# Splitting the next stage's first weights early, storing the residual tile by tile, and reordering the first norm, in a one-core hybrid decoder layer

## The chip, the cores and the metric

The kernel runs on one core of a Trainium2 chip, as a single program. The metric is the device time of one execution in microseconds (us). A core has five engines that matter here: PE (TensorE, matrix products), DVE (VectorE), ACT (ScalarE), POOL (GpSimd) and SP (SyncE, which in this kernel issues nearly all DMAs). Each engine takes its instructions in order; semaphores tie the engines together.

## The reference

The reference is one inference step of one decoder layer for 576 tokens: a prompt of 512 and eight samples of 8 tokens. The model width D is 1024, the feed-forward width 2816. In fp32 it computes

- `x = x + 1/2 * SwiGLU_1(rmsnorm(x))`, where `SwiGLU(h) = (silu(h @ w_gate) * (h @ w_up)) @ w_down`;
- `h = rmsnorm(x)`, `P = h @ w_in`: one projection that gives queries, keys and values of a dilated sliding-window attention (branch A) and of a gated linear attention (branch B), an output gate `rg` for B, and one gate for each branch;
- `m = sigmoid(g_a) * (A @ w_a_out) + sigmoid(g_b) * (B @ w_b_out)`, then `x = x + m @ w_out`;
- `x = x + 1/2 * SwiGLU_2(rmsnorm(x))`, and the new rows of the key-value caches and the new GLA states as further outputs.

`rmsnorm(x)` is `x * rsqrt(mean(x*x) + eps) * g`, row by row. B's output is multiplied by `silu(rg)`.

## The kernel before

**Tiling.** The residual x is kept transposed in SBUF: `xT` is 128 x 8 x 576, eight tiles of 128 features, and the 576 tokens are two HALVES of 288. A "group" is one output tile of 128 features for one half: eight k tiles, each with three matmuls of 128 x 128 by 128 x 288, so 24 matmuls. The three matmuls stand for one fp32 product: every fp32 operand is split into a high part (a cast to fp32r) and a low part (what the cast lost), and `feat_mm` adds high x high (L191), high x low (L192) and low x high (L193). Where the tokens are the rows of the result, L921 to L923 do the same (`ptok`). The larger part of the feed-forward products runs as `Unit`s, a Strassen scheme of seven half-size products (`Unit.products`, L521 to L523, results `pX`, `pY`, `pZ`).

**Weights.** A weight tile of 512 KB goes through `fetch_w` (DMA from SP's queue, L160, into a buffer `raw`), then `split`: ACT casts it (`wh`, L138), DVE subtracts (`wl`, L139). PE's L191 needs `wh`, its L193 needs `wl`. The buffers belong to a pool that is opened for each stage by `weights(raw_bufs, w_bufs, sums)`: 4 and 6 in the sublayers, 2 and 8 in the mixer and in the `w_out` loop. A new stage's pool lies where the old one lay, so its first fetch waits for what the old stage does there.

**Norms.** The 1/rms of a token is a factor of the whole row, so the products start with `x * g` (`operand`, L228 on ACT for the high and L229 on DVE for the low part) and each result is multiplied by `row`, which holds 1/rms of each token along the free axis. For a norm between stages `updated` runs for each (tile, half) of x as it becomes final: operand, square (L236, L238) and running sum (L239). After the sixteenth, `sums` adds over the partitions by matmuls with ones (`pssq`, L250), takes mean plus eps on DVE (`rms`, L207) and the power -1/2 on POOL (`rtok`, L208), and `rows_` spreads it by transposes on PE (`prow`, L221) and copies by ACT (`row`, L222).

**Order.** PE's order is the order of the code (the kernel is written under a manual schedule); a scheduler orders the other engines' instructions when the program is built. A small helper, `weave`, counts PE's groups: `weave.put_off(n, step)` puts a step n groups later, `weave.tick()` closes a group, and `weave.run` interleaves lists of groups and steps.

**Stages.** (1) *Start*: x is loaded as tokens x features, transposed by PE (`first_tokens`), the first norm's squares are summed per token (`first_squares`: chunks 0 to 2 by ACT at L333, 3 to 5 by DVE at L335), the root comes from POOL (`st`, L208), `first_rows` makes `row`. (2) *First sublayer*, `sublayer(E, xT, 1, ...)`: 16 groups of class `First` (mat 0 is gate, 1 is up; `evac` multiplies by `row` at L615 and L619, takes silu at L616 and the product at L621), while `normal_steps` makes the normed operands of the `Unit`s (`factor` at L575; L585, L586 and L591 combine them; `hop` are the split results); then `Unit`s for gate, up and down, and at the end `Last` groups (`pd`) whose results are added to x at L740 and handed to `after1`. When all sixteen are there, SP stores x to DRAM (`xsp`, L392) in two transfers, since the mixer needs the room. (3) *Mixer*: it opens with three tiles of the gate `rg`, all of half 0 first, then all of half 1 (`feat_groups`, results `pf`, evacuated by DVE at L966, two groups later); then attention (first result `ptok`), gated linear attention and the branches. ACT's silu of a gate tile (L994) needs both halves of it. (4) *`w_out` loop*: x is reloaded from `xsp`, eight tiles of `w_out` (results `pwo`) are added at L415 and go to `updated`. (5) *Second sublayer*, as the first, with its own weights, and output.

Of the kernel before, what the change touches and what calls it, by code (L numbers as in the profile page):

```python
# [9 lines left out]
F32 = mybir.dt.float32  # L10
# [88 lines left out]
def hybrid_step_kernel(  # L99
# [199 lines left out]
    for c in range(3, 6):  # L299
        load_x(c)  # L300

    fst = xi.tile([NC, 24], F32, tag="st1", name="st1", bufs=1)

    def first_columns():
        pc = ps_bg("pcols1")
# [23 lines left out]

    def first_squares(c):  # L330
        sq = xi.tile([NC, D], F32, tag="sqx", name="sqx", bufs=1)
        if c < 3:
            S.activation(sq, xt[c], AF.Square, accum_out=fst[:, c:c + 1])  # L333
        else:
            V.tensor_tensor_reduce(sq, xt[c], xt[c], op0=ALU.mult, op1=ALU.add, scale=1.0, scalar=0.0,  # L335
                                   accum_out=fst[:, c:c + 1])
        if c % 3 == 2:
            rstd_of(fst[:, 14 + c:17 + c], fst[:, c - 2:c + 1], fst[:, 6 + c:9 + c], D)

# [26 lines left out]
    def second():  # L366
        for c in range(3, 6):
            first_tokens(c)
        wpre[0, 1] = load_w([gv[:, :, P:2 * P]])
        for c in range(3):  # L370
            first_squares(c)

    weave.put_off(1, second)
    weave.put_off(2, lambda: first_operands(1))
    weave.put_off(2, lambda: [first_squares(c) for c in range(3, 6)])
    weave.put_off(4, lambda: (first_rows(0), E.scaled(0)))

    def last_rows():
        first_rows(1)
        start.close()  # L380
        other_columns()
        xin.close()
        E.scaled(1)

    weave.put_off(5, last_rows)
    seen = []

    def after1(m, h):
        updated(xT, m, h, 2, sacc[:, :T], sacc[:, T:], seen)
        if len(seen) == 2 * KD:  # L390
            for s in HALVES:
                SP.dma_start(xsp[:, :, s], xT[:, :, s])  # L392

    sublayer(E, xT, 1, ffn1_gate, ffn1_up, ffn1_down, wpre, after1)
    sub.close()
    wst.close()
    wst = weights(2, 8)
    mxs = ExitStack()
    mixer(E, mxs, bk, xpool)
    bk = banks(6)  # L400
    branches(E, mxs)

# [5 lines left out]
    ov = kview(w_out)  # L408
    for m in range(KD):
        w = load_w([ov[:, :, m * P:(m + 1) * P]])  # L410
        for h, s in enumerate(HALVES):
            po = ps_acc("pwo")
            feat_mm(po[:, :HALF], w, 0, P, E.mH, E.mL, range(KD), s)
            weave.tick()
            V.tensor_add(xT[:, m, s], po[:, :HALF], xT[:, m, s])  # L415
            updated(xT, m, h, 3, sacc[:, :T], sacc[:, T:], seen)
# [22 lines left out]
            q.dma_start(y_prompt[0, SEQ - 32:SEQ, c], y[:32, 2 * P:])  # L439
            q.dma_start(ys[:, c], y[32:, 2 * P:])  # L440

    sublayer(E, xT, 3, ffn2_gate, ffn2_up, ffn2_down, {}, lambda m, h: weave.put_off(1, lambda: out(m, h)))
    weave.finish()
    sub.close()
    wst.close()
# [78 lines left out]
        self.done(i, ps)  # L524


def sublayer(E, xT, g, wg, wu, wd, wpre, after):


    V, S, weave = E.V, E.S, E.weave  # L530
# [28 lines left out]
    normed = []  # L559

    def scaled(*halves):
        ready.update(halves)
        if len(ready) == 2:
            E.scaled = lambda *halves: None
            weave.put_off(1, normal)

    def normal():

# [31 lines left out]
        normed.extend((fn, k) for k in range(4) for fn in (lower, lower2, lower3))  # L600

    def normal_steps(n):
        for fn, *a in normed[:n]:
            fn(*a)
        del normed[:n]

    E.scaled = scaled
    ps = {}
# [41 lines left out]
            E.feat_mm(po[:, :HALF], wpre[mat, f], 0, P, E.hH, E.hL, range(KD), HALVES[h])  # L650
            waiting.append((mat, f, h, weave.at + 2))

    first = [First(*k) for k in ((0, 0, 0), (1, 0, 0), (0, 1, 0), (0, 0, 1), (1, 0, 1), (1, 1, 0), (0, 1, 1), (1, 1, 1))]
    first += [First(mat, f, h) for f in range(2, 2 * FIRST) for mat in range(2) for h in range(2)]


    def gate(pair):
# [87 lines left out]

    units = [fn(pair) for pair in phases[0][FIRST:] for fn in (gate, up)]
    for n, phase in enumerate(phases):
        nxt = phases[n + 1] if n + 1 < len(phases) else tail
        units.append(gate(nxt[0]))
        downs = [down(phase, m) for m in range(0, KD, 2)]  # L750
        rest = [up(nxt[0])] + [fn(pair) for pair in nxt[1:] for fn in (gate, up)]
        units += rest + downs if nxt is tail else downs + rest
    lasts = [Last(m) for m in range(0, KD, 2)]

    slots = [(-1, u, 0) for u in first]
# [30 lines left out]
    for i, (_, u, n) in enumerate(slots):  # L786
        ahead(i)
        u.products(n)
        weave.tick()
        evacuate(i)  # L790
        normal_steps(2)
        if not any(isinstance(x[1], Unit) for x in slots[i + 1:]):
            for x in final:
                after(*x)
            final.clear()
# [136 lines left out]
    return [loaded(load, group, t) for t in range(5)]  # L932


def feat_groups(E, c0, ms, evac, by_half=False):

    wv = E.kview(E.w_in)
    ws = {}

    def load(m, h):  # L940
        if m not in ws:
            ws[m] = E.load_w([wv[:, :, c0 + m * P:c0 + (m + 1) * P]])

    def group(m, h):
        s = HALVES[h]
        po = E.ps_acc("pf")
        E.feat_mm(po[:, :HALF], ws[m], 0, P, E.hH, E.hL, range(KD), s)
        if by_half:
            E.weave.put_off(2, lambda: evac(m, s, po[:, :HALF]))
        else:  # L950
            evac(m, s, po[:, :HALF])

    order = [(m, h) for h in range(2) for m in ms] if by_half else [(m, h) for m in ms for h in range(2)]
    return [loaded(lambda a=a: load(*a), group, *a) for a in order]


def mixer(E, mxs, bk, xpool):
    S, weave = E.S, E.weave
    E.mxl = mxs.enter_context(E.sb("mixl"))
    E.aH = E.mxl.tile([P, 2, T], F32R, name="aH")  # L960
# [4 lines left out]
    E.oT = oT = [E.slot(E.slotsA, F32, f"oT{m}") for m in range(KD)]  # L965
    gate_out = lambda m, s, ps: E.V.tensor_mul(oT[m][:, s], ps, E.row[:, s])  # L966

    weave.run(feat_groups(E, C_RG, range(3), gate_out, True))
    xpool.close()
    bk.close()  # L970
    bk = E.banks(4)
# [723 lines left out]
```

## Time and profile before

| what | value |
|---|---|
| median of 3 runs | 1450.68 us (1449.65 to 1452.04) |
| the profiled execution | 1450.8 us, its span 1449.0 us |
| PE busy | 1406.5 us, 97% of the span |
| DVE busy | 1066.9 us, 74% |
| ACT busy | 720.8 us, 50% |
| POOL busy | 58.7 us, 4% |
| DMA | 144.26 MB, mean 100 GB/s |
| mean granted PE clock | 0.989 of full speed |

The span is the time from the first to the last recorded instruction; the execution's own time has a little more around it. A row of the timeline gives the start in us, the duration, the engine, the line of the kernel, what is written and read, and in brackets the idle time of the engine before it with what ended it. A row of a window gives its bounds and length, the busy time of each engine with the number of instructions, the granted clock of PE as a share of full speed, the DMA engines' busy share and what they moved.

### The profile page before, as it was taken

How to read it: one execution, taken by the hardware profiler on the slowest of the kernel's cores; microseconds unless marked ns; L12 is line 12 of the kernel's file. 1: busy time of each engine (PE TensorE's matmuls, PEld its weight loads, DVE VectorE, ACT ScalarE, POOL GpSimd, SP SyncE). 2: the span in 40 equal slices, each digit the busy share in tenths (PEclk: the TensorE clock that was granted, in tenths of full speed). 3: DMA queues.
4: the chain of work that ended last, by engine and by line, in shares of the span. 5: the costliest groups of instructions: out<-in, count | busy, mean ns of one | idle time of the engine just before them, and what ended most of it. 6: DMA issues, size and time to landing. Idle time of an engine off the chain costs nothing.

```text
span 1449.0 us, 27438 instructions
## 1 busy us (share of the span) xinstructions
PE 1406.5 (97%) x10836; PEld 1374.3 (95%) x10836; DVE 1066.9 (74%) x2340; ACT 720.8 (50%) x1468; POOL 58.7 (4%) x89
## 2 busy tenths in 40 slices
PE   7989999999969999999999999999999999999998
PEld 7979999999959999998999999999999999999997
DVE  6999999998844456542477666555479999999892
ACT  6564664665533455632455644323345556556642
POOL 2000000000012212000000000000000000000000
PEclk9999999999979999999999999999999999999999
DMA  7223323332252442273324432325221333233232
GB/s 194 61 63 99 102 78 114 88 102 78 70 155 82 139 128 72 73 200 121 88 63 118 123 110 81 84 81 167 74 80 53 92 114 88 88 104 101 83 109 66
DMA packets 179951, 144.26 MB, mean 100 GB/s; under 512 B 7242, under 2 KB 178944, under 8 KB 179824
## 3 DMA queue, kind: packets, MB, share of 16 engines
q1 hardware_dynamic: 179488, 142.34, 33.7%
q8 instruction: 85, 1.39, 0.4%
q0 software_dynamic: 336, 0.18, 0.1%
q14 instruction: 42, 0.34, 0.1%
HBM read 128.72 MB, written 13.78 MB: 98 GB/s over the span
## 4 chain that ended last, share of the span: by engine, by line
PE 90%; DVE 5%; DMA 2%; ACT 1%; SPq 1%; issue 0%; POOL 0%; ACTq 0%; POOLq 0%; DVEq 0%
PE pX L523 8%; PE pX L522 8%; PE pX L521 8%; PE pY L522 4%; PE pY L523 4%; PE pY L521 4%; PE pf L191 4%; PE pf L193 3%; PE pf L192 3%; PE ptok L921 3%; PE ptok L923 3%; PE ptok L922 3%; PE pZ L522 2%; PE pZ L523 2%; PE pZ L521 2%; PE pg L191 1%
## 5 line engine op out<-in xcount | busy, mean ns | idle before, releaser
L138 ACT CAST w<-raw 128x512 fp32r<-128x512 f32 (+1 forms) x360 | 205.4, 578 | 123.6 <-PE pX L523 32.3
L139 DVE TENSOR_TENSOR w<-raw,w 128x512 fp32r<-128x512 f32 (+1 forms) x360 | 224.6, 635 | 21.1 <-ACT w L138 18.9
L521 PE MATMUL pX<-hop,w 128*128 128x288 f32 x576 | 170.1, 295 | 5.0 <-ACT w L138 5.0
L523 PE MATMUL pX<-hop,w 128*128 128x288 f32 x576 | 171.0, 297 | 3.0 <-DVE w L139 3.0
L522 PE MATMUL pX<-hop,w 128*128 128x288 f32 x576 | 170.8, 297 | 0.0
L138 ACT CAST wh<-raw 128x1024 fp32r<-128x1024 f32 (+2 forms) x111 | 106.7, 969 | 124.6 <-PE pf L192 46.6
L139 DVE TENSOR_TENSOR wl<-raw,wh 128x1024 fp32r<-128x1024 f32 (+2 forms) x111 | 124.0, 1125 | 46.2 <-ACT wh L138 45.7
L191 PE MATMUL pf<-h,wh 128*128 128x288 f32 x384 | 119.2, 310 | 13.9 <-ACT wh L138 13.9
L921 PE MATMUL ptok<-wl,h 128*128 128x256 f32 x416 | 120.1, 289 | 0.0
L923 PE MATMUL ptok<-wh,h 128*128 128x256 f32 x416 | 116.9, 281 | 0.0
L922 PE MATMUL ptok<-wh,h 128*128 128x256 f32 x416 | 116.7, 281 | 0.0
L193 PE MATMUL pf<-h,wl 128*128 128x288 f32 x384 | 114.8, 299 | 0.4 <-DVE wl L139 0.4
L192 PE MATMUL pf<-h,wh 128*128 128x288 f32 x384 | 114.6, 299 | 0.0
L521 PEld LDWEIGHTS pX<-hop,w 128*128 128x128 f32 x576 | 109.1, 189 | 5.7 <-ACT w L138 5.7
L523 PEld LDWEIGHTS pX<-hop,w 128*128 128x128 f32 x576 | 109.0, 189 | 4.3 <-DVE w L139 4.3
L522 PEld LDWEIGHTS pX<-hop,w 128*128 128x128 f32 x576 | 109.1, 189 | 0.0
L191 PEld LDWEIGHTS pf<-h,wh 128*128 128x128 f32 x384 | 73.9, 192 | 17.0 <-ACT wh L138 14.1
L522 PE MATMUL pY<-hop,w 128*128 128x288 f32 x288 | 85.1, 296 | 0.0
L523 PE MATMUL pY<-hop,w 128*128 128x288 f32 x288 | 85.0, 295 | 0.0
L521 PE MATMUL pY<-hop,w 128*128 128x288 f32 x288 | 84.6, 294 | 0.0
L191 PE MATMUL pg<-h,wh 128*128 128x288 f32 x256 | 79.1, 309 | 3.2 <-ACT wh L138 2.4
L921 PEld LDWEIGHTS ptok<-wl,h 128*128 128x128 f32 x416 | 78.6, 189 | 1.8 <-issue 1.3
(426 smaller groups left out, 4268.9 us busy)
## 6 DMA issues: line engine op xcount, KB each, us to landing
raw<-in_w_in_dram SPq DMA_DIRECT2D x58, 512.0 KB, 3.9
raw<-in_ffn_gate_dram SPq DMA_DIRECT2D x45, 512.0 KB, 3.8
raw<-in_ffn_up_dram SPq DMA_DIRECT2D x44, 512.0 KB, 3.8
raw<-in_ffn_down_dram SPq DMA_DIRECT2D x48, 384.0 KB, 3.2
raw<-in_ffn_down_dram SPq DMA_DIRECT2D x8, 512.0 KB, 3.6
kv<-in_cache_swa_kv_dram SPq DMA_DIRECT2D x32, 128.0 KB, 4.0
kv<-in_cache_swa_kv_dram SPq DMA_DIRECT2D x16, 256.0 KB, 4.3
S<-in_state_gla_dram SPq DMA_DIRECT2D x4, 1024.0 KB, 6.8
```

The lines of the kernel that those rows point to most:

```text
L138: S.copy(hi, src)
L139: V.tensor_sub(lo, src, f32(hi))
L191: PE.matmul(ps, h, ah, start=first and j == 0, stop=False)
L192: PE.matmul(ps, h, al, start=False, stop=False)
L193: PE.matmul(ps, l, ah, start=False, stop=last and j == n - 1)
L521: PE.matmul(ps, wh[:, k], ah, start=opens and k == 0, stop=False, skip_group_check=True)
L522: PE.matmul(ps, wh[:, k], al, start=False, stop=False, skip_group_check=True)
L523: PE.matmul(ps, wl[:, k], ah, start=False, stop=k == self.nk - 1, skip_group_check=True)
L921: PE.matmul(po[:, :256], ah, wl, start=(k == 0), stop=False)
L922: PE.matmul(po[:, :256], al, wh, start=False, stop=False)
L923: PE.matmul(po[:, :256], ah, wh, start=False, stop=(k == KD - 1))
```

## The change

It has five parts.

1. *Start*: the sums of squares lie in `sacc` instead of a tile of their own; all six squares are ACT's; the second half's operands come in two pieces, before and after squares 0 to 2; squares 3 to 5 are put off by three groups, and the second half's row by six instead of five.
2. *Residual*: `after1` stores each (tile, half) of x as soon as it is final, 16 stores of 144 KB from POOL's queue (L394 of the changed kernel), instead of two stores of 1152 KB from SP's queue after all of them.
3. *Mixer's first weights*: within the first sublayer's `Last` groups, after tiles 2 and 4, the weights of gate tiles 0 and 1 are fetched and split, in the sublayer's pool. The mixer then runs tile 0 and 1 half by half (four groups), and tile 2 behind them with both halves in a row; its weight is loaded from the mixer's pool.
4. *Second sublayer's first weights*: in the last round of the `w_out` loop the first gate and the first up weight are fetched and split, in that stage's pool.
5. *Order in the sublayers*: the normed operands' steps start as soon as the first half's row is there (those that need only this half), and the order of the `First` groups puts both matrices of one half next to each other; the first sublayer keeps its first eight.

```diff
-    fst = xi.tile([NC, 24], F32, tag="st1", name="st1", bufs=1)
+    fst = sacc[:NC, :24]
...
     def first_squares(c):
         sq = xi.tile([NC, D], F32, tag="sqx", name="sqx", bufs=1)
-        if c < 3:
-            S.activation(sq, xt[c], AF.Square, accum_out=fst[:, c:c + 1])
-        else:
-            V.tensor_tensor_reduce(sq, xt[c], xt[c], op0=ALU.mult, op1=ALU.add, scale=1.0, scalar=0.0,
-                                   accum_out=fst[:, c:c + 1])
+        S.activation(sq, xt[c], AF.Square, accum_out=fst[:, c:c + 1])
...
         wpre[0, 1] = load_w([gv[:, :, P:2 * P]])
+        first_operands(1, range(4))
         for c in range(3):
             first_squares(c)
-
-    weave.put_off(1, second)
-    weave.put_off(2, lambda: first_operands(1))
-    weave.put_off(2, lambda: [first_squares(c) for c in range(3, 6)])
-    weave.put_off(4, lambda: (first_rows(0), E.scaled(0)))
-
-    def last_rows():
-        first_rows(1)
-        start.close()
+        first_operands(1, range(4, KD))
+
+    def squares():
+        for c in range(3, 6):
+            first_squares(c)
         other_columns()
         xin.close()
+
+    def first_half():
+        first_rows(0)
+        start.close()
+        E.scaled(0)
+
+    def second_half():
+        first_rows(1)
         E.scaled(1)
 
-    weave.put_off(5, last_rows)
+    weave.put_off(1, second)
+    weave.put_off(3, squares)
+    weave.put_off(4, first_half)
+    weave.put_off(6, second_half)
     seen = []
 
     def after1(m, h):
         updated(xT, m, h, 2, sacc[:, :T], sacc[:, T:], seen)
-        if len(seen) == 2 * KD:
-            for s in HALVES:
-                SP.dma_start(xsp[:, :, s], xT[:, :, s])
-
-    sublayer(E, xT, 1, ffn1_gate, ffn1_up, ffn1_down, wpre, after1)
+        G.dma_start(xsp[:, m, HALVES[h]], xT[:, m, HALVES[h]])
+
+    wmix, wi = {}, kview(w_in)
+
+    def mixer_weights(m):
+        wmix[m] = load_w([wi[:, :, C_RG + m * P:C_RG + (m + 1) * P]])
+
+    sublayer(E, xT, 1, ffn1_gate, ffn1_up, ffn1_down, wpre, after1, mixer_weights, True)
...
-    mixer(E, mxs, bk, xpool)
+    mixer(E, mxs, bk, xpool, wmix)
...
         w = load_w([ov[:, :, m * P:(m + 1) * P]])
+        if m == KD - 1:
+            wpre = {(i, 0): load_w([v[:, :, 0:P]]) for i, v in enumerate((kview(ffn2_gate), kview(ffn2_up)))}
...
-    sublayer(E, xT, 3, ffn2_gate, ffn2_up, ffn2_down, {}, lambda m, h: weave.put_off(1, lambda: out(m, h)))
+    sublayer(E, xT, 3, ffn2_gate, ffn2_up, ffn2_down, wpre, lambda m, h: weave.put_off(1, lambda: out(m, h)))
...
     def scaled(*halves):
+        if not ready:
+            normal()
         ready.update(halves)
         if len(ready) == 2:
             E.scaled = lambda *halves: None
-            weave.put_off(1, normal)
...
     def normal_steps(n):
-        for fn, *a in normed[:n]:
+        while n and normed and (len(normed[0]) == 3 or 1 in ready):
+            fn, *a = normed.pop(0)
             fn(*a)
-        del normed[:n]
+            n -= 1
...
-    first = [First(*k) for k in ((0, 0, 0), (1, 0, 0), (0, 1, 0), (0, 0, 1), (1, 0, 1), (1, 1, 0), (0, 1, 1), (1, 1, 1))]
-    first += [First(mat, f, h) for f in range(2, 2 * FIRST) for mat in range(2) for h in range(2)]
+    order = [(mat, f, h) for f in range(2 * FIRST) for h in range(2) for mat in range(2)]
+    if late:
+        order[2:6] = (0, 1, 0), (0, 0, 1), (1, 0, 1), (1, 1, 0)
+    first = [First(*k) for k in order]
...
         weave.tick()
+        if isinstance(u, Last) and n == 3 and u.m in (2, 4):
+            nxt(u.m // 2 - 1)
         evacuate(i)
...
-    ws = {}
+    ws = {} if ws is None else ws
...
-    weave.run(feat_groups(E, C_RG, range(3), gate_out, True))
+    weave.run(feat_groups(E, C_RG, range(2), gate_out, True, ws) + feat_groups(E, C_RG, [2], gate_out))
```

The scheduler gives ACT, DVE and POOL new orders. Three places follow; a row is line, operation, what is written and read, shape and number of like instructions.

First place, ACT at the start of the mixer (`aup` and `lw` are small weights of the gated linear attention, `wh` the high part of a weight, `oT` the gate's tiles, whose silu is L994 before and L1010 after). Before:

```order
444 L973 CAST hS<-h_62 128x8x64
445 L238 ACTIVATE sacc_128<-xT 128x288
446 L1380 CAST aup<-up 32x512 x2
447 L138 CAST wh<-raw 128x1024 x2
448 L1373 CAST lw_7789<-lw 128x8x16
449 L138 CAST wh<-raw 128x1024 x2
450 L222 COPY row<-prow 128x512
451 L222 COPY row<-prow 128x64
452 L138 CAST wh<-raw 128x1024
453 L994 ACTIVATE oT_5066<-oT_5066 128x576
```

After:

```order
446 L238 ACTIVATE sacc_128<-xT 128x288
447 L1389 CAST lw_7802<-lw 128x8x16
448 L1396 CAST aup<-up 32x512 x2
449 L222 COPY row<-prow 128x512
450 L222 COPY row<-prow 128x64
451 L1010 ACTIVATE oT_5091<-oT_5091 128x576
452 L989 CAST hS<-h_62 128x8x64
453 L1010 ACTIVATE oT_5092<-oT_5092 128x576
454 L138 CAST wh<-raw 128x1024 x4
```

The casts of the first two weights have moved ahead of this place, into the first sublayer; the cast of the third now stands behind the row's copies and behind the silu of tiles 0 and 1.

Second place, ACT at the start of the second sublayer (`sg` and `g` are the gate's results, `up` and `hop` the normed operands of the `Unit`s before and after their split). Before:

```order
868 L138 CAST wh<-raw 128x1024 x3
869 L222 COPY row<-prow 128x512
870 L222 COPY row<-prow 128x64
871 L616 ACT_TABLE_LOAD
872 L616 ACTIVATE sg<-sg 128x288
873 L138 CAST hop<-up 128x288 x4
874 L138 CAST g_12330<-sg 128x288
875 L616 ACTIVATE sg<-sg 128x288
876 L138 CAST hop<-up 128x288
877 L138 CAST wh<-raw 128x1024
```

After:

```order
869 L222 COPY row<-prow 128x512
870 L222 COPY row<-prow 128x64
871 L628 ACT_TABLE_LOAD
872 L628 ACTIVATE sg<-sg 128x288
873 L138 CAST hop<-up 128x288 x4
874 L138 CAST g_12355<-sg 128x288
875 L628 ACTIVATE sg<-sg 128x288
876 L138 CAST hop<-up 128x288 x4
877 L138 CAST wh<-raw 128x1024
```

Before, three weights were cast ahead of the row and a fourth behind five operand casts; now two are cast in the stage before, and the third, which is that of group E (the fifth, gate tile 1), stands behind eight operand casts.

Third place, DVE at the start (L335 are its squares, L207 mean plus eps, L575 before and L586 after the normed operands). Before:

```order
28 L207 TENSOR_SCALAR st_166<-st_166 96x3
29 L229 SCALAR_TENSOR_TENSOR h_62<-xT,cols,h_62 128x288 x8
30 L335 ISA sqx,st_166<-xtok 96x1024
31 L335 ISA st_166 96x1
32 L335 ISA sqx,st_166<-xtok 96x1024
33 L335 ISA st_166 96x1
34 L575 SCALAR_TENSOR_TENSOR up<-xT,cols,row 128x288
35 L335 ISA sqx,st_166<-xtok 96x1024
```

After:

```order
28 L229 SCALAR_TENSOR_TENSOR h_62<-xT,cols,h_62 128x288 x4
29 L207 TENSOR_SCALAR sacc_128<-sacc_128 96x3
30 L229 SCALAR_TENSOR_TENSOR h_62<-xT,cols,h_62 128x288 x4
31 L207 TENSOR_SCALAR sacc_128<-sacc_128 96x3
32 L312 COPY cols<-pcols 128x22
33 L313 TENSOR_SCALAR cols<-pcols 128x3
34 L139 TENSOR_TENSOR wl<-raw,wh 128x1024
35 L627 TENSOR_TENSOR sg<-pg,row 128x288
```

The three squares have left DVE, and the statistics of the second half (row 31) now wait for ACT's squares.

More of the change, by code (lines that the diff above doesn't have):

```diff
@@ L524, in products, with sublayer @@
         self.done(i, ps)
-def sublayer(E, xT, g, wg, wu, wd, wpre, after):
+def sublayer(E, xT, g, wg, wu, wd, wpre, after, nxt=lambda m: None, late=False):
     V, S, weave = E.V, E.S, E.weave
@@ L747, in sublayer @@
     for n, phase in enumerate(phases):
-        nxt = phases[n + 1] if n + 1 < len(phases) else tail
-        units.append(gate(nxt[0]))
+        then = phases[n + 1] if n + 1 < len(phases) else tail
+        units.append(gate(then[0]))
         downs = [down(phase, m) for m in range(0, KD, 2)]
-        rest = [up(nxt[0])] + [fn(pair) for pair in nxt[1:] for fn in (gate, up)]
-        units += rest + downs if nxt is tail else downs + rest
+        rest = [up(then[0])] + [fn(pair) for pair in then[1:] for fn in (gate, up)]
+        units += rest + downs if then is tail else downs + rest
     lasts = [Last(m) for m in range(0, KD, 2)]
@@ L932, in tok_groups, with feat_groups @@
     return [loaded(load, group, t) for t in range(5)]
-def feat_groups(E, c0, ms, evac, by_half=False):
+def feat_groups(E, c0, ms, evac, by_half=False, ws=None):
     wv = E.kview(E.w_in)
-    ws = {}
+    ws = {} if ws is None else ws
     def load(m, h):
@@ L954, in feat_groups, with mixer @@
     return [loaded(lambda a=a: load(*a), group, *a) for a in order]
-def mixer(E, mxs, bk, xpool):
+def mixer(E, mxs, bk, xpool, ws):
     S, weave = E.S, E.weave
```

## The prediction

> **What bounds the kernel now.** I read the shares, then TensorE's waits, then the stretches around them. A first fence has one line of the page and four groups of PE's waits (us in total, times, longest).
>
> ```profile
> PE 1406.5 (97%) x10836; PEld 1374.3 (95%) x10836; DVE 1066.9 (74%) x2340; ACT 720.8 (50%) x1468; POOL 58.7 (4%) x89
> PE pf L191 <- ACT wh L138: 13.9, 1, 13.9
> PE pX L521 <- ACT w L138: 5.0, 3, 4.2
> PE pg L191 <- ACT wh L138: 2.4, 1, 2.4
> PE prow L221 <- POOL st L208: 2.2, 1, 2.2
> ```
>
> TensorE is busy for 97%, and the change removes no matmul. So only PE's holes and the slow clock behind them can be won, and they lie at three seams: the program's start (4.2 and 2.2), first sublayer to mixer (13.9), `w_out` to second sublayer (2.4). The profiled execution took 1450.8 us, its span 1449.0; 1.8 lie around it, and it is 0.1 above the median of 1450.7. I sum against the span and add 1.8.
>
> **Term 1: first sublayer to mixer.** Rows of the timeline (start, us, engine, line, [idle before <- what ended it]), the last two from the next seam:
>
> ```profile
> 406.35 0.30 PE L193 MATMUL pd<-hop,wl 128*128 128x288 f32 x1
> 420.50 0.61 PE L191 MATMUL pf<-h,wh 128*128 128x288 f32 x1 [13.85 <-ACT wh L138]
> 445.09 0.28 PE L921 MATMUL ptok<-wl,h 128*128 128x256 f32 x1
> ...
> 406.12 1.59 SPq L392 DMA_DIRECT2D xsp<-xT  x2
> 419.41 1.04 ACT L138 CAST wh<-raw 128x1024 fp32r<-128x1024 f32 x1 [3.24 <-DMA raw<-in_w_in_dram]
> 420.48 1.23 DVE L139 TENSOR_TENSOR wl<-raw,wh 128x1024 fp32r<-128x1024 f32 x1 [4.25 <-ACT wh L138]
> ...
> 1062.74 0.79 PE L221 MATMUL prow<-ident,rtok 128*128 128x128 f32 x5
> 1063.47 0.40 PE L191 MATMUL pg<-h,wh 128*128 128x288 f32 x1
> 1108.16 0.29 PE L521 MATMUL pX<-hop,w 128*128 128x288 f32 x1
> ```
>
> SP issues the two residual stores (406.12), then the first weight; that lands at 419.4, ACT casts it for 1.04 and PE starts at 420.50. A full-speed group of 24 matmuls costs 3.19: 14 of them fill 1063.47 to 1108.16. From the last product's slot end (406.35 + 0.13, call it B = 406.48) to the first `ptok` at 445.09 are 38.6. Six groups need 19.1, the row transposes 0.73 (1062.74 to 1063.47), the five sums some 0.6 (estimate: as many small matmuls): 20.4. So 18.2 are lost now.
>
> After the change the weights of tiles 0 and 1 are fetched and split inside the first sublayer's last quarter, so four groups start at B. What the casts cost there: two times 1.04 on ACT and 1.23 on DVE, in the second of these windows (us; busy us and instructions of PE, PEld, DVE, ACT, POOL; granted clock; DMA share; GB/s); the first is from the `w_out` loop:
>
> ```profile
> 1000.00:1040.00 40.00, 40.00 (x304) 40.00 (x303) 20.86 (x41) 14.21 (x28) 0.00 (x0) 1.00 0.41 126
> 390.00:400.00 10.00, 10.00 (x78) 10.00 (x77) 8.39 (x21) 5.58 (x13) 0.00 (x0) 1.00 0.00 0
> ...
> 409.09 0.58 POOL L861 DMA_DIRECT2D gk<-in_a_k_norm_dram  x1
> 428.56 1.24 POOL L208 TENSOR_TENSOR rtok<-rms,mhalf 128x5 f32<-128x5 f32 x1 [18.89 <-DVE rms L207]
> 435.69 0.46 DVE L966 TENSOR_TENSOR oT<-pf,row 128x288 f32<-128x288 f32 x1 [2.15 <-PE pf L193]
> 439.71 0.68 ACT L994 ACTIVATE oT<-oT 128x576 f32<-128x576 f32 x1
> ```
>
> Room is there (DVE 8.4 of 10, ACT 5.6, DMA idle), so I cost it at nothing; without that cover DVE's 2 x 1.23 would be late on PE's last groups. The same holds for the two pairs that the third edit splits in the `w_out` loop (DVE 20.9 of 40, ACT 14.2), at most 2.5 if they fell behind the last group's evacuation. The start's sums kept in `sacc` instead of a tile of their own are free: nothing else writes there until the first sublayer's end. The 16 residual stores ride POOL's queue at about 0.58 each (row `gk`); they too are hidden as long as POOL is free before it must compute `rtok` (1.24), which the row transposes need at B + 2 x 3.19 + 0.6 = B + 7.0.
>
> But a new wait appears. The order shows ACT's third weight behind the silu of tile 1's output (first place in the part on the change). That silu needs both halves of tile 1, that is group 4, which ends at B + 4 x 3.19 + 1.3 = B + 14.1. Then L982 (0.46), its L1010 (0.68), the cast (1.04): PE's `L191` of group 5 comes at +2.4 and its `L193` with the subtraction 1.2 later. Loss of time: 2.45 + some 0.95 (1.2 less the slot that PE works meanwhile) = 3.4. Behind such a wait the clock drops; that this happens after a hole of 2.4 the second seam shows:
>
> ```profile
> 1048.95 0.29 PE L193 MATMUL pwo<-mH,wl 128*128 128x288 f32 x1
> 1051.62 0.61 PE L191 MATMUL pg<-h,wh 128*128 128x288 f32 x1 [2.38 <-ACT wh L138]
> 1052.88 0.61 PE L193 MATMUL pg<-h,wl 128*128 128x288 f32 x1 [0.41 <-DVE wl L139]
> 1051.95:1058.78 6.83, 6.42 (x29) 6.07 (x28) 3.15 (x3) 1.51 (x2) 0.00 (x0) 0.52 0.73 199
> ```
>
> In 6.83 us 29 matmuls ran, worth 3.86 at 0.133: 2.97 lost, 0.4 of it the wait for `wl`, so 2.6 for the clock. The new stall costs 3.4 + 2.6 = 6.0 to 6.1. **Gain 18.2 - 6.1 = 12.1.** Bounds: 18.2 if ACT is never late; with stall and slow clock twice that long, 6.
>
> A rule stands beside the clock: the Trainium skill ("TensorE: Matmul & The Clock Gate", Part 1, HAM) says the array is throttled after an idle window of about 3.4 us and that a kernel must keep idle gaps below that. Here 2.38 us of idle already brought 0.52, so the trace is harsher than the rule. By the rule the new stall of 2.45 would keep full clock, and the sum would be 2.6 better, near 1434; I go by the rows.
>
> **Term 2: `w_out` to second sublayer.** With B' = 1049.08 (1048.95 + 0.13) the third group starts at 1063.47 now: 14.4, for two groups, sums and transposes (7.7); 6.7 lost. After the change the first two weights are split in the previous stage's buffers, and its first four groups A to D run through to B' + 14.1, the row standing 6.7 earlier. Then the fifth, E, waits: on ACT its weight's cast (row 877, second place) stands behind eight operand casts. DVE and ACT rows:
>
> ```profile
> 1064.00 0.46 DVE L615 TENSOR_TENSOR sg<-pg,row 128x288 f32<-128x288 f32 x1 [4.25 <-ACT row L222]
> 1064.73 1.80 DVE L575 SCALAR_TENSOR_TENSOR up<-xT,cols,row 128x288 f32<-128x288 f32 x4
> 1065.74 1.42 ACT L138 CAST hop<-up 128x288 fp32r<-128x288 f32 x4
> ...
> PE pX L523 <- DVE w L139: 1.1, 2, 0.7
> PE pX L521 <- ACT w L138: 0.4, 1, 0.4
> ```
>
> DVE starts 1.26 after the transposes (1064.00 - 1062.74): B' + 8.2. About 20 steps of 0.37 to 0.45 (1.80 / 4) bring it to the eighth `up` at B' + 16.5, behind group D's evacuation at 14.3 to 14.7; cast 0.36 (1.42 / 4), then 1.05: PE's E at B' + 17.9 and its `wl` at 19.6 instead of 14.3. Loss 5.3 + 2.6 for the clock = 7.9, so PE reaches the first Strassen unit (now 1108.16) 1.2 later. DVE, however, which sets the pace there (the two wait rows, 1.5 together, are of 1100 to 1122), began 6.7 earlier and loses one `wl` and its own waits from this; I put it 1.8 ahead. Then the 1.5 vanish: **gain 0.2**, between -1.2 (no stall vanishes) and 5.6 (E not late: 6.7 less the 1.1 of a further `wl`).
>
> **Term 3: the start.** Squares 3 to 5 move from DVE to ACT, operands are cut in two, other products come first.
>
> ```profile
> 20.25 1.06 ACT L333 ACTIVATE sqx<-xtok 96x1024 f32<-96x1024 f32 x1
> 23.67 3.51 ACT L228 ACTIVATE h<-xT,cols 128x288 fp32r<-128x288 f32 x8
> 27.66 1.22 DVE L335 CUSTOM_DVE_ANT_0 sqx<-xtok 96x1024 f32<-96x1024 f32 x1
> 32.32 1.76 POOL L208 TENSOR_TENSOR st<-st,mhalf 96x3 f32<-96x3 f32 x1 [7.39 <-DVE st L207]
> 37.48 0.46 DVE L621 TENSOR_TENSOR sg<-s,sg 128x288 f32<-128x288 f32 x1 [2.41 <-ACT sg L616]
> 76.43 0.69 DVE L497 TENSOR_TENSOR raw<-raw 128x512 f32<-128x512 f32 x1
> 78.78 0.60 PE L521 MATMUL pX<-hop,w 128*128 128x288 f32 x1 [4.16 <-ACT w L138]
> 36.00:72.00 36.00, 36.00 (x267) 36.00 (x266) 34.52 (x84) 20.18 (x43) 0.00 (x0) 0.97 0.22 64
> ```
>
> DVE is full (34.5 of 36), and PE's 4.16 at 78.78 ends with DVE's `L497` chain. What counts is when DVE starts its long run: now with `L621` at 37.48. Three squares of 1.22 leave it (third place), but ACT must then do them (3 in 23.67 - 20.25 = 3.4, after operands for 3.51), so second-half statistics come at 31.1, the next cast at 32.1, DVE's `wl` at 33.3 and its first `L633` at 35.2. That is 2.3 earlier; one more `wl` ahead of `L506` takes 0.4 of it back. PE loses the 2.2 of `prow` and gains about 4.6 at weight (0,3), whose subtraction sits late in DVE's order; it reaches its units at 75 to 76, still before DVE lets it go on. **Gain 1.9**, bounds -0.8 (PE at 79.6 instead of 78.8) and 4.2 (the whole hole).
>
> **The sum.** 1449.0 - 12.1 - 0.2 - 1.9 = 1434.8; with 1.8 it is 1436.6, so **1436.5**. The likeliest case's own range is 1432.5 to 1440.5.
>
> **Rivals.** *E in time*: DVE reaches the eighth `up` before group D ends. For it: bunched DVE steps run at 0.37; against it: twenty must fit in under 5 us. Term 2 becomes 5.6: 1431. *Third mixer weight in time*: the order holds but the silu isn't late, or PE's half-speed is spared; term 1 becomes 18.2: 1430.5. It speaks against it that the silu needs group 4. *Start gives nothing*: the wait at (0,3) takes the place of the 4.2; against it, DVE is ahead. Term 3 becomes -0.8: 1439.2.
>
> *POOL late, slower than before.* The residual stores are in order ahead of `rtok` on POOL, along with a memset and two more DMA issues:
>
> ```profile
> 406.71 1.38 POOL L1011 MEMSET Qm<- 128x1536 f32 x1 [64.42 <-PE pd L193]
> 408.04 1.07 POOL L1378 DMA_DIRECT2D up<-in_g_alpha_up_dram  x2
> L740 DVE TENSOR_TENSOR xT<-pd,xT x32: 446/458/459, 379.2 to 1442.2; 128x288 f32<-128x288 f32 x32
> ```
>
> The stores become ready one per product group, 16 from 379.2 to 406.7, 1.75 apart. With X per store, `rtok` is there at 379.7 + 16 X + 1.38 + 1.07 + 1.24; B + 7.0 = 413.5 allows X = 1.88. Above that each 0.1 delays the row by 1.6; at 2.76 the gain of 14.2 is gone (16 x 0.88 = 14.1), at 3.1 the time is 1436.5 + 19.5 = 1456. For it: DVE is busy for 8.4 of 10 there. Against it: the only POOL issues seen, beside a working DVE or not, took 0.53 to 0.58.
>
> The Trainium skill speaks against this edit: "SBUF — State Buffer", the box on the DVE-blocks-DMA trap in "SBUF: two separate sides" says that a DMA issued from GpSimd needs descriptors that GpSimd can't write while DVE runs a two-port operation, and a later section gives about 0.62 us alone and 3.1 overlapped. By the larger figure the sum would be near the 1456 above; no run so far shows it, and the same page excludes it for operations of two tensors, which most of DVE's are here.
>
> **How the numbers follow.** Forecast 0.58; E in time 0.12; third weight in time 0.09; start nothing 0.08; POOL late 0.13, of which 0.08 slower than before, 0.03 level, the rest below it. A measurement tells about 0.2% (2.9 us) from no change. Faster: 0.58 + 0.12 + 0.09 + 0.08 + 0.02 = 0.89; same 0.03; slower 0.08. The range 1428 to 1443 takes in the first four cases and leaves out the late POOL and both good cases together (1425).
>
> **What would show it.** Right: no 13.85 at the first `pf`, a wait of about 2.4 at the fifth `pf` group behind ACT's cast, the clock near 0.5 behind it, `ptok` at about B + 26; in the second seam no wait before A, one of 3 to 4 at E; `prow` of the start without its 2.2, and 4 to 5 at (0,3). Wrong: `prow` in the mixer waiting for POOL, stores of over 1.9 each, the casts in the last quarter delaying `pd`, or matmuls that run slower in the stretch of the stores.

## The result and the profile after

The changed kernel takes 1441.1 us (median of 6 runs, 1439.8 to 1443.2) against 1450.7 of the kernel before: a ratio of 0.9931, with a 95% interval of 0.9916 to 0.9946. The profiled execution, the slowest of the six, took 1443.2 us with a span of 1440.7. On the page PE's share has risen by little:

```profile
PE 1409.5 (98%) x10836; PEld 1377.9 (96%) x10836; DVE 1063.6 (74%) x2334; ACT 724.0 (50%) x1474; POOL 66.5 (5%) x105
```

PE's waits (us in total, times, longest), the rows that answer to the 13.9, 5.0, 2.4 and 2.2 of before:

```profile
PE pg L193 <- DVE wl L139: 6.5, 3, 4.9
PE pg L191 <- ACT wh L138: 3.6, 1, 3.6
PE pf L191 <- ACT wh L138: 2.2, 1, 2.2
PE pX L532 <- DVE w L139: 2.1, 2, 1.7
PE pf L193 <- DVE wl L139: 0.7, 1, 0.7
```

The 13.9 and the 2.2 at `prow` are gone. New are 2.2 + 0.7 in the mixer, 3.6 + 1.2 in the second sublayer and 4.9 in the start. The places, in PE's timeline of the changed kernel:

```profile
61.57 0.61 PE L193 MATMUL pg<-h,wl 128*128 128x288 f32 x1 [4.91 <-DVE wl L139]
...
378.93 0.29 PE L191 MATMUL pd<-hop,wh 128*128 128x288 f32 x1
...
407.99 0.29 PE L191 MATMUL pf<-h,wh 128*128 128x288 f32 x1
...
425.12 0.40 PE L191 MATMUL pf<-h,wh 128*128 128x288 f32 x1 [2.20 <-ACT wh L138]
426.38 0.40 PE L193 MATMUL pf<-h,wl 128*128 128x288 f32 x1 [0.73 <-DVE wl L139]
...
434.12 0.28 PE L937 MATMUL ptok<-wl,h 128*128 128x256 f32 x1
...
1042.25 0.29 PE L191 MATMUL pg<-h,wh 128*128 128x288 f32 x1
1060.84 0.40 PE L191 MATMUL pg<-h,wh 128*128 128x288 f32 x1 [3.62 <-ACT wh L138]
1062.53 0.61 PE L193 MATMUL pg<-h,wl 128*128 128x288 f32 x1 [1.16 <-DVE wl L139]
1102.14 0.29 PE L530 MATMUL pX<-hop,w 128*128 128x288 f32 x1
```

The first mixer group starts in the very slot behind the last down product (407.99), and `ptok` comes 26.1 later instead of 38.6. The second sublayer's first four groups start without a hole too, but its first Strassen unit comes 59.9 behind the seam (1102.14 - 1042.25), against 59.1 before.

Stage by stage, between the same instructions in the two profiles: up to the first down product (`pd`, 377.43 before, 378.93 now) 1.5 lost; seam to the mixer 12.5 gained; from the first `ptok` to the `w_out` loop 4.1 lost; from there to the last down products 1.5 gained; together 8.4; the spans differ by 8.3. PE has no wait in the 4.1 by the profile. They are the clock, as PE's windows show (us; busy us and instructions of PE, PEld, DVE, ACT, POOL; granted clock; DMA share; GB/s), the first row from the kernel before and the rest from the changed one, all in the gated linear attention and with the same matmuls:

```profile
667.89:998.21 330.32, 330.32 (x2586) 314.50 (x2585) 192.41 (x392) 145.07 (x255) 12.66 (x23) 1.00 0.34 99
...
656.60:991.37 334.77, 334.77 (x2585) 318.45 (x2584) 192.32 (x392) 145.11 (x255) 12.66 (x23) 0.98 0.34 98
720.21:723.63 3.42, 3.42 (x20) 2.77 (x20) 0.91 (x2) 1.05 (x4) 0.00 (x0) 0.63 0.92 252
761.17:764.59 3.42, 3.42 (x20) 2.77 (x20) 0.91 (x2) 0.97 (x4) 0.00 (x0) 0.63 1.10 336
764.59:768.00 3.41, 3.41 (x16) 3.41 (x16) 0.00 (x0) 0.08 (x1) 0.00 (x0) 0.50 0.92 258
```

### The profile page after: what moved, and what is told of

Same layout as the page of the kernel before. It is cut to its first block, busy times and chain, and to the rows that moved or that the text cites. A ratio compares the mean times of both kernels' runs of the same rounds, so it can differ in the third digit from the quotient of the medians.

```text
span 1440.7 us, 27488 instructions
## 1 busy us (share of the span) xinstructions
PE 1409.5 (98%) x10836; PEld 1377.9 (96%) x10836; DVE 1063.6 (74%) x2334; ACT 724.0 (50%) x1474; POOL 66.5 (5%) x105
## 4 chain that ended last, share of the span: by engine, by line
PE 92%; DVE 4%; ACT 1%; DMA 1%; SPq 1%; issue 0%; POOL 0%; DVEq 0%; ACTq 0%; POOLq 0%
PE pX L532 8%; PE pX L531 8%; PE pX L530 8%; PE pY L531 4%; PE pY L532 4%; PE pY L530 4%; PE pf L191 4%; PE pf L193 4%; PE pf L192 3%; PE ptok L937 3%; PE ptok L939 3%; PE ptok L938 3%; PE pZ L531 2%; PE pZ L532 2%; PE pZ L530 2%; PE pg L193 2%
## 5 line engine op out<-in xcount | busy, mean ns | idle before, releaser
L193 PE MATMUL pg<-h,wl 128*128 128x288 f32 x256 | 78.4, 306 | 6.5 <-DVE wl L139 6.5
```

Source lines behind the costliest of these rows:

```text
L193: PE.matmul(ps, l, ah, start=False, stop=last and j == n - 1)
```

## The experiments

The first four take the change apart. **The mixer's part alone**: stores from GpSimd's queue and early weights, the rest as before.

```diff
-        if len(seen) == 2 * KD:
-            for s in HALVES:
-                SP.dma_start(xsp[:, :, s], xT[:, :, s])
+        G.dma_start(xsp[:, m, HALVES[h]], xT[:, m, HALVES[h]])
...
+    sublayer(E, xT, 1, ffn1_gate, ffn1_up, ffn1_down, wpre, after1, mixer_weights, True)
...
+    weave.run(feat_groups(E, C_RG, range(2), gate_out, True, ws) + feat_groups(E, C_RG, [2], gate_out))
```

> Only the residual's stores from GpSimd's queue and the mixer's two early weights are added to the kernel before; start, order of the first products and second sublayer are as before. My theory: the seam from the first sublayer to the mixer gives all of the gain: from the last down product to the first ptok 26.1 us instead of 38.6, as in the changed kernel, so about 1450.7 - 12.5 = 1438.2, faster than the full change. Rival 'the parts help each other' (the start's new order is needed for room on DVE at the end of the first sublayer): a gain under 9, 1442 or more.

Measured: 1439.6 (1438.4 to 1444.9), ratio 0.9927 with 0.9910 to 0.9943. That is 11.8 less than the 1451.5 of the kernel before beside it (12.5 were expected), as much as the whole change brings. The rival "the parts help each other" falls.

**The second sublayer's part alone**: its early weights, its order of first products, its normed operands (`late` marks the first sublayer, which keeps the old rules).

```diff
+            wpre = {(i, 0): load_w([v[:, :, 0:P]]) for i, v in enumerate((kview(ffn2_gate), kview(ffn2_up)))}
...
+        if not ready and not (late):
+            normal()
...
+    if late:
+        order = [(0, 0, 0), (1, 0, 0), (0, 1, 0), (0, 0, 1), (1, 0, 1), (1, 1, 0), (0, 1, 1), (1, 1, 1)]
+        order += [(mat, f, h) for f in range(2, 2 * FIRST) for mat in range(2) for h in range(2)]
```

> Only the second sublayer's two early weights and its new order of first products and normed operands are added to the kernel before. By the traces (59.9 us instead of 59.1 to the first Strassen unit, then 2.4 less) the stage gains 1.5: 1449.2, a wait of 3.6 for the fifth group's cast and 1.2 for its low part, and no wait of the first Strassen units. The prediction's term was 0.2: 1450.5. Rival 'fifth group in time': 1445.

Measured: 1451.8 beside 1451.5, ratio 0.9999 with 0.9988 to 1.0009. PE's waits from 1040 to 1125 us are 3.6 as expected and 0.8 for 1.2, and the units have none:

```profile
PE pg L191 <- ACT wh L138: 3.6, 1, 3.6
PE pg L193 <- DVE wl L139: 0.8, 1, 0.8
```

The holes have only moved. The 1449.2 read off one trace was too good; the 0.2 of the prediction lies within the interval, which runs from 1.7 less to 1.3 more.

**The start alone**: all six squares on ACT, the put-off steps and the order of the first sublayer.

```diff
+    fst = sacc[:NC, :24]
...
+        S.activation(sq, xt[c], AF.Square, accum_out=fst[:, c:c + 1])
...
+    weave.put_off(3, squares)
+    weave.put_off(4, first_half)
+    weave.put_off(6, second_half)
```

> Only the start is changed: six squares on ACT, operands in two pieces, the rows later, the new order of the first sublayer's products. By the trace of the full change the start loses: the wait of 4.9 at gate tile 3 and the waits of 1.65, 0.40 and 0.43 with a slow clock behind them; the first down product comes 1.0 later than before if loading is equal: 1451.7. The prediction's term was a gain of 1.9: 1448.8. Rival 'only the loading of x was late in that one profile': no change, 1450.7.

Measured: 1452.1 beside 1451.5, ratio 1.0002 with 0.9993 to 1.0011. The interval runs from 1.0 less to 1.6 more: no gain of 1.9, and no clear loss either. Sums of windows from 12 to 92 us show where the work went, first before, then this kernel:

```profile
sum 80.00, PE 70.12 PEld 68.19 DVE 72.41 ACT 48.64 POOL 2.64; mean PE 17.53 PEld 17.05 DVE 18.10 ACT 12.16 POOL 0.66
```

```profile
sum 80.00, PE 70.72 PEld 69.13 DVE 69.39 ACT 52.09 POOL 1.74; mean PE 17.68 PEld 17.28 DVE 17.35 ACT 13.02 POOL 0.43
```

Three squares of 1.22, 3.7 us, have left DVE, but DVE has worked 3.0 less in the same time: it was idle for that long more. What it waited for, before and in this kernel:

```profile
DVE sg L621 <- ACT sg L616: 2.4, 1, 2.4
DVE st L207 <- ACT sqx L333: 2.1, 1, 2.1
DVE wl L139 <- ACT wh L138: 1.9, 1, 1.9
```

```profile
DVE sacc L207 <- ACT sqx L332: 5.3, 2, 2.9
DVE wl L139 <- ACT wh L138: 3.3, 2, 2.7
DVE sg L630 <- ACT sg L625: 0.9, 1, 0.9
```

DVE waits 5.3 for ACT's squares where it waited 2.1: the work changed its engine, and the engine with the bound waits for it. The 3.3 for weight casts are another matter. 2.7 of them stand ahead of the squares, at a cast that itself waited for its weight, and that weight came 1.1 later than in the other execution; only 0.6 stands behind the squares. The rows, each time before and then this kernel:

```profile
16.86 1.04 ACT L138 CAST wh<-raw 128x1024 fp32r<-128x1024 f32 x1 [1.69 <-DMA raw<-in_ffn_gate_dram]
90.87 0.45 DVE L669 TENSOR_TENSOR sg<-sg,pX 128x288 f32<-128x288 f32 x1
...
17.99 1.05 ACT L138 CAST wh<-raw 128x1024 fp32r<-128x1024 f32 x1 [2.45 <-DMA raw<-in_ffn_gate_dram]
91.07 0.45 DVE L683 TENSOR_TENSOR sg<-sg,pX 128x288 f32<-128x288 f32 x1
```

The instruction near 91 us is the same one in both, and this kernel reaches it 0.2 later. Counted from the cast of that weight it is 0.9 ahead.

**The whole again, beside its parts** (no edit).

> The full change again, on the same chip as its parts. If the parts add up, its time is that of before less 12.5 and 1.5 and plus 1.0, so 13.0 less; the traced run was 4 slower than that since the clock fell to 0.63 and 0.50 in two stretches of the gated linear attention near 721 and 762 us, without a wait of TensorE. If that fall belongs to the change, it is in this run's profile again and the parts exceed the whole by 4; if it comes by chance, it is gone or elsewhere, and the time is near 1438 to 1440.

Measured: 1440.7 (1439.3 to 1442.2), ratio 0.9926 with 0.9913 to 0.9939. The parts (11.8 less, 0.4 more, 0.6 more by the medians) make 10.8 less, the whole 10.8 less: they add up. The two falls of the clock near 721 and 762 are not there; one other is, near 841 (331.82 us for the stage instead of 330.32), so where they come differs between executions of one kernel.

The next two split the mixer's part. **The stores alone**:

```diff
-        if len(seen) == 2 * KD:
-            for s in HALVES:
-                SP.dma_start(xsp[:, :, s], xT[:, :, s])
+        G.dma_start(xsp[:, m, HALVES[h]], xT[:, m, HALVES[h]])
```

> The kernel before with one edit: the residual is stored tile by tile from GpSimd's queue; the mixer's weights are loaded as before, in the mixer's own buffers, all three in half-by-half order. Theory A (the 13.85 is a wait for bandwidth behind 2.3 MB of stores, 259 GB/s in that stretch): without them the first weight is there early, its cast starts when ACT has done its operands and squares, some 3 us behind the last down product, PE waits 4 instead of 13.85, then a second wait and the slow clock as before: a gain of 9 to 10, about 1442. Theory B (the early split alone brings the gain, the stores are only moved): a gain under 3, 1448 or more.

Measured: 1440.2, ratio 0.9934 with 0.9918 to 0.9950, 10.3 less than the kernel before beside it. PE's waits and SP's rows:

```profile
PE pf L191 <- ACT wh L138: 3.0, 1, 3.0
PE pf L193 <- DVE wl L139: 0.7, 1, 0.7
...
376.39 1.20 SPq L160 DMA_DIRECT2D raw<-in_ffn_down_dram  x2
378.91 12.65 SPq L160 DMA_DIRECT2D raw<-in_w_in_dram  x2
407.98 0.37 SPq L1370 DMA_DIRECT2D lw<-in_w_in_dram  x1
```

The wait of 13.85 has shrunk to 3.05, without any early split. The two weights' fetches are issued at 378.9 and 391.2, ahead of the sublayer's end; before, they stood on SP behind two stores that waited 29.9 for the last tiles of x (issued at 406.12). Theory B falls; theory A has the size right, but not the whole cause: the stores cost the fetches their place in the queue as well as bandwidth. Once issued (the first at 407.8) they took 11.8 to land beside the stores, here 3.9 and 5.1. This run takes both away at once; by these numbers (11.8 less 4.5) some 7 of the 10.8 won at this wait would be bandwidth, an estimate that no run tests. The 3.05 left is ACT's own work ahead of the cast: from 408.48 to 411.89 it is busy for 3.38.

**The early weights alone**, stores as before (against the mixer's part):

```diff
-        G.dma_start(xsp[:, m, HALVES[h]], xT[:, m, HALVES[h]])
+        if len(seen) == 2 * KD:
+            for s in HALVES:
+                SP.dma_start(xsp[:, :, s], xT[:, :, s])
```

> The kernel before with the other half of that change: the mixer's first two weights are split early, the residual leaves in two stores from SP's queue at the end as before. Theory A says that here too nearly all of the gain remains, since four groups cover 14 us, and the third weight, which shares the DMA engines with the stores as before and lands some 12.5 behind the last down product, is cast behind the silu of tile 1 anyway: a gain of 11 to 12.5, 1439 to 1440.5; the small weight up, cast by ACT ahead of the row, may land late and take 1 of it. Theory B' (both parts are needed): a gain under 8.

Measured: 1438.9, ratio 0.9923 with 0.9908 to 0.9937, 11.5 less than before; PE's waits there are again 2.2 and 0.7. Either half brings nearly all, and the two do not add; which of the three kernels is the fastest the intervals don't say.

Then the waits that the change left. **The mixer's first six groups in the code's order on all engines** (on top of the mixer's part alone):

```diff
-    weave.run(feat_groups(E, C_RG, range(2), gate_out, True, ws) + feat_groups(E, C_RG, [2], gate_out))
+    with E.tc.manual_schedule():
+        weave.run(feat_groups(E, C_RG, range(2), gate_out, True, ws) + feat_groups(E, C_RG, [2], gate_out))
```

> The first experiment (stores and early weights alone) with all engines held to the code's order for the mixer's first six groups, so that the third weight's cast stands ahead of both silus on ACT and its subtraction ahead of the third and fourth evacuation on DVE. If the 2.2 and 0.73 at the fifth pf group come from that place on ACT, both waits go (its low part overlies tile 0's weight, which is free at 10.9 behind the last down product, so it is ready at 12.3, ahead of the 14.1 needed), and with them the slow clock behind: 20.4 to 21 from the last down product to ptok instead of 26.1, 5 to 6 less than the first experiment: 1433.5 to 1434.5. If the third weight is really held by its buffer or its transfer until the fourth group ends, the waits stay and the time with them, 1439.6.

Measured: 1433.0 (1432.5 to 1433.6), ratio 0.9877 with 0.9861 to 0.9894, clear of both kernels. From 407.43 to 428.56, 21.1 us, PE has no wait and full clock, and ACT casts the third weight 3.5 ahead of the first silu:

```profile
407.43:428.56 21.13, 21.13 (x162) 20.86 (x161) 11.32 (x26) 9.84 (x16) 5.22 (x7) 1.00 0.46 126
...
417.62 1.06 ACT L138 CAST wh<-raw 128x1024 fp32r<-128x1024 f32 x1
421.10 0.69 ACT L1010 ACTIVATE oT<-oT 128x576 f32<-128x576 f32 x1 [0.85 <-DVE oT L981]
```

So the 2.2 came from the cast's place on ACT, as the prediction read it from the order, and the third weight's transfer was there in time. From the last down product to `ptok` it is 21.1 instead of the 26.0 of the mixer's part alone, so 4.9 less; by the medians, each against the kernel before beside it, 5.7 (17.5 less instead of 11.8).

**The second sublayer's second to fourth group in the code's order** (on top of the whole change):

```diff
+    byhand = ExitStack()
     for i, (_, u, n) in enumerate(slots):
+        if not late and i == 1:
+            byhand.enter_context(E.tc.manual_schedule())
+        if i == 4:
+            byhand.close()
         ahead(i)
```

> The full change with the engines held to the code's order for the second sublayer's second to fourth group, so that on ACT the fifth group's weight is cast behind two operand casts instead of eight. The waits of 3.63 and 1.14 at the fifth group go, with the slow clock behind them. The rival of the prediction made 5.4 of it (DVE alone sets the pace, started earlier): 1435.3. My theory now: DVE was idle for only 2.6 between the row and the first Strassen units in the full change, so it cannot gain more than that, and the units wait for it instead: a gain of 1 to 2.6, 1438 to 1439.7.

Measured: 1437.7 (1434.5 to 1439.1), ratio 0.9908 with 0.9892 to 0.9923, about 3 less than the whole change measured in the other sets of runs, which doesn't pin it down closer. The fifth group no longer waits; 1.25 and 1.04 stand at the sixth, and the units wait for DVE again, as the theory had it:

```profile
PE pg L193 <- DVE wl L139: 1.5, 2, 1.0
PE pg L191 <- ACT wh L138: 1.2, 1, 1.2
PE pX L532 <- DVE w L139: 0.7, 1, 0.7
```

**The two joined**, with the start of before: the mixer's part and the second sublayer's part, and

```diff
+    with E.tc.manual_schedule():
+        weave.run(feat_groups(E, C_RG, range(2), gate_out, True, ws) + feat_groups(E, C_RG, [2], gate_out))
...
+        if not late and i == 1:
+            byhand.enter_context(E.tc.manual_schedule())
+        if i == 4:
+            byhand.close()
```

> Three edits joined: stores and early weights at the mixer, the mixer's six groups in the code's order, and the second sublayer of the last experiment (early weights, second to fourth group in the code's order); the start is that of the kernel before. If the gains add up: 1433.0 of the mixer in the code's order, less 2.0 to 2.4 (the stage from w_out to the last down products, 406.3 instead of 408.3 to 408.7), so 1430.6 to 1431. If the second sublayer's gain was chance of the clock in that one run, 1433.

Measured: 1432.8 (1432.2 to 1435.5), ratio 0.9877 with 0.9860 to 0.9893: level with the mixer's edit alone. In the profiles the stage from `w_out` to the last down products is 406.3 (982.39 to 1388.70) instead of the 408.3 of the mixer's edit alone, but one fall of the clock in the gated linear attention (331.82 us instead of 330.31) took 1.5 of it back. That the 2.0 are worth having isn't shown.

**Two groups more in the code's order** in the second sublayer, against the kernel just told of:

```diff
-        if i == 4:
+        if i == 6:
             byhand.close()
```

> The same with two groups more in the code's order in the second sublayer, so that the sixth group's weight too is cast behind four operand casts instead of behind eight. It takes away the waits of 1.25 and 1.04 that were left there. If DVE sets the pace, the Strassen units wait for that time instead and nothing is gained or up to 0.5 lost by its steps held back: the time of the kernel beside it, within 1. If PE's own waits count, 2 less.

Measured: 1440.2 (1436.9 to 1441.6), 7.4 slower than its neighbour, outside both expectations; by the profiles the stage from `w_out` to the last down products takes 412.5 instead of 406.3. PE's waits and DVE's waits from the seam on:

```profile
PE pX L528 <- DVE w L139: 4.6, 4, 2.4
PE pX L526 <- ACT w L138: 0.9, 2, 0.5
...
DVE hop L139 <- ACT hop L138: 3.3, 5, 1.3
DVE wl L139 <- ACT wh L138: 2.1, 3, 1.1
```

In its neighbour DVE waits 1.8 and 0.5 in those rows. In the code's order DVE and ACT hand each split to and fro, DVE stands for 3 us more, and 40 us later the units wait for it (4.6 instead of 0.8), with a slow clock there (0.85 from 1090 to 1110). My theory had the bound right and the price of holding it back wrong.

**GpSimd's queue made late**: two small powers behind each store, on top of the mixer's part alone.

```diff
         G.dma_start(xsp[:, m, HALVES[h]], xT[:, m, HALVES[h]])
+        for i in range(2):
+            G.tensor_tensor(rtok, ones.to_broadcast([P, 5]), xT[:, m, h * HALF:h * HALF + 5], op=ALU.pow)
```

> The first experiment (stores and early weights alone), with two small powers on GpSimd behind each store, of about 1.3 us each, so that a store costs that queue 0.54 + 2.6 = 3.1 us instead of 0.54. The prediction's rival: up to 1.88 it is free, above it each 0.1 delays the row by 1.6. At 3.1 the row's root ends near 435 instead of 414, PE waits some 20 at the row's transposes with a slow clock behind, and the time is 1459 to 1463, slower than before. If the row isn't on the path, the time stays at 1440.

Measured: 1463.2 in two executions, ratio 1.0083 with 1.0060 to 1.0106. The rival's price for the row was right, 19.2 of waiting for 16 x (3.1 - 1.88) = 19.5:

```profile
PE prow L221 <- POOL rtok L208: 19.2, 1, 19.2
PE pf L191 <- ACT wh L138: 2.2, 1, 2.2
```

The time rose by more, 23.5 over the mixer's part alone when each is taken against the kernel before beside it; behind the wait the clock was 0.64 (433.4 to 440.2 us), which the prediction's 1456 had left out and the expectation of this run had in.

## Why the prediction was right, and where not

*The mixer (term 1, 12.1): right in size and mechanism.* Measured: 12.5 in the profiles and 11.8 in the part alone. The new wait stood where the order put it (2.20 for 2.4, then 0.73 for 1.2), the clock fell behind it, and the experiment in the code's order took all of it away; the 21.1 us that were left are near the 20.4 of the working. The rival "third mixer weight in time" was thus a matter of order and worth 4.9 in the profiles and 5.7 by the medians, where the prediction said 6.

*What it did not see:* that the two halves of this edit cover for each other. It costed the early split as the gain and the stores as free. Stores alone give 10.3, split alone 11.5, both 11.8.

*Costs at nothing.* The late casts cost nothing on PE's last groups: the first `pf` follows the last `pd` without a gap, and from the first `pd` to there it is 29.1 us as before. GpSimd's stores took mostly 0.54 each (0.58 was taken; the 0.53 to 0.58 said to be all issues seen overlooked the kernel's start, where they took 0.52 to 0.70) with DVE at work beside them, and its root waited for DVE's `rms`, not the other way:

```profile
399.40 1.07 POOL L394 DMA_DIRECT2D xsp<-xT  x2 [2.66 <-DVE xT L754]
412.59 1.35 POOL L208 TENSOR_TENSOR rtok<-rms,mhalf 128x5 f32<-128x5 f32 x1 [0.95 <-DVE rms L207]
```

The rival "POOL late" therefore did not come. None of the 16 took over 0.64, while DVE was busy for 25.4 of 30.3 us (379.7 to 410). The Trainium skill ("SBUF — State Buffer", "A bandwidth-pool intuition that's wrong") gave 3.1 for a store overlapped with a DVE copy, which did not come here. The case of operations with two tensors, which the same page leaves out of the trap ("Who interferes with whom"), is the one that these runs show.

*The second sublayer (term 2, 0.2): right.* The part alone is 0.9999. The wait at the fifth group was forecast as 3.6 for the cast (17.9 - 14.3) and measured as 3.62. The 1.5 that one pair of profiles gives this stage is scatter: from `w_out` to the last down products it takes 408.3 to 409.2 in seven profiles with the old second sublayer, and 407.7 to 408.7 in three with the new one. The rival "E in time" was mispriced: with the fifth group in time the stage takes 406.3, 1.4 to 2.4 less, not the 5.4 between the two terms. That DVE had only 2.6 of idle time left there is the likely reason.

*The start (term 3, 1.9): wrong.* The step that failed is "what counts is when DVE starts its long run". The run did start earlier: L633 at 35.8 in the changed kernel (35.2 was forecast) for the same step, L621, at 37.48 before. But part of the work that DVE had done before 37.48 was still ahead of it, and DVE had waited longer for ACT on the way. Near 91 us DVE of the part alone is 0.2 behind the kernel before, the first down product comes at 377.63 for 377.43, and the part measures 1.0002. One thing stays open. Counted from the cast of the first large weight, the start is 0.9 ahead near 91 us; that cast came at 17.5 to 18.0 in the four profiles with the new start and at 16.8 to 17.9 in the nine with the old, and whether the change makes it later isn't shown. PE's wait of 4.91 at gate tile 3 was forecast at 4.6 and, as forecast, took the place of others: PE's waits from 25 to 95 us are 8.2 in the part alone for 8.6 before. The rival "start gives nothing" came true here.

*The sum.* 14.2 were forecast and 9.6 measured (1441.1; 10.8 in the second set of runs). By the medians of the parts alone (11.8 less, 0.4 more, 0.6 more) the start is 2.5 of the 3.4 that were missing in the second set, the other two terms 0.3 and 0.6. The 1.2 between the two sets isn't explained: executions of one kernel differ by some 6 us with the granted clock, and 4.1 of that lay in the profiled one. The range, 1428 to 1443, held it; the narrower one of the likeliest case, to 1440.5, did not hold the 1441.1. With a third term of nothing, the same working would have said 1438.4.

## What to carry to other kernels

When an engine waits for a transfer at a seam, look first at what stands ahead of that transfer in its queue: two stores that waited for the last result held up two loads, the first of which could go out 28.9 us earlier (378.9 for 407.8), and then shared the DMA engines with them; moving either side took most of the wait away. Read the order of the engines around a wait that is to go: what the scheduler puts ahead of the next weight's cast was visible before any run, and worth about half of what the change itself brought. Work that is moved off a bound engine need not gain anything: here that engine then waited for its result. Holding engines to the code's order is no rule either: at the mixer it won 4.9, and two groups too many in the second sublayer cost 7.4.

## What the runs showed of the hardware

The clock falls without a wait. In the gated linear attention PE is never idle by the profile, yet the stage took 330.31, 331.82, 333.29 or 334.77 us in different executions, in steps of 1.5: the shortest at full clock throughout, the others with one or two falls to between 0.5 and 0.9 in windows of 3.4 us:

```profile
650.87:984.16 333.29, 333.29 (x2585) 317.16 (x2584) 192.38 (x392) 145.08 (x255) 12.66 (x23) 0.99 0.34 98
```

The falls have a place. Four times in the stage PE runs small products for some 4 us (`pdiag`, and `pcross` with 128 x 32), and each fall begins within 1 us of the end of one of these stretches: the first two in the changed kernel, the fourth in its second profile, the second in the mixer's part alone, the first in the kernel with two groups more, the fourth in the two joined. The end of the first stretch in the changed kernel, and a large product behind it that takes 0.44 instead of 0.29:

```profile
720.36 0.77 PE L1509 MATMUL pcross<-qe,kc 128*32 128x32 f32 x6
...
722.66 0.44 PE L192 MATMUL pf<-h,wh 128*128 128x288 f32 x1
```

The kernel before ran the same four stretches at full clock, so why a fall comes behind some and not others stays open. Kernels with and without the change show it (the slowest executions of the kernel before, 1455, have a mean clock of 0.987, the fastest 0.991). One profiled execution was 3.2 us off the median of its kernel (1434.5 for 1437.7), so a gain of one or two us can't be read from a single pair of profiles.

A hole of 2.2 us, followed by one of 0.73, is enough for a slow clock:

```profile
428.00:431.40 3.40, 3.40 (x17) 3.40 (x17) 0.30 (x1) 1.05 (x1) 0.00 (x0) 0.56 0.84 275
```

The Trainium skill ("TensorE: Matmul & The Clock Gate", Part 1) puts the fall behind about 3.4 us of idleness; here 2.2 and 0.73, 2.9 in all, brought it. With the holes taken away the same stretch ran at 1.00 and was 4.9 us shorter.
